# Both MLP products of a two-layer decoder trunk by seven block products each, with the intermediate in HBM

## The chip, the cores and the metric

The kernel runs on one core of a Trainium2 chip, as one launch. The metric is device microseconds from the first to the last instruction, as the median of several executions. The engines are PE (TensorE, matmuls), DVE (VectorE), ACT (ScalarE), POOL (GpSimd) and SP (SyncE, which issues most DMAs). SBUF is the on-chip memory with 128 partitions, PSUM the accumulator memory of TensorE with eight banks, HBM the memory outside the core.

## What is computed

The reference is a trunk of two layers on one sequence of 16 meta tokens and 1024 tokens, D = 1024 features, D_FF = 4096. The first layer (A) has stick-breaking attention, the second (B) differential attention. Each ends in an MLP, and only the MLPs matter here:

```python
def rmsnorm(x, g):
    y = x * lax.rsqrt(jnp.mean(x * x, axis=-1, keepdims=True) + EPS)
    return y * g
...
def squared_relu_mlp(x, g, w_in, w_out):
    h = rmsnorm(x, g)
    return jnp.square(jax.nn.relu(h @ w_in)) @ w_out
...
h = h + squared_relu_mlp(h, mlp_norm_g[layer], mlp_w_in[layer], mlp_w_out[layer])
```

Layer A has 1040 tokens, layer B 1024, since the meta tokens are dropped at the end. All data are float32.

## The kernel before

The stream is kept feature-major (features on partitions, tokens along the free axis) in three chunks of tokens: 400, 384 and 256 in layer A (`CH`), 384, 384 and 256 in layer B (`BCH`). Every product is made in three passes of a faster float format (`mm3`): each operand is split into a high part (`acopy`, a cast on ACT, line 99) and a low part (`tt(..., subtract)`, on DVE, line 113), and high·high, high·low and low·high add up in one PSUM bank (`mm`, line 159). Other helpers are `stt` (line 117, DVE), `ptt` (line 121, an add or subtract on POOL) and `rstd_from` (a matmul with ones, a square root and a reciprocal on line 207).

An MLP is `mlp()`. `out_proj` before it adds the attention's output projection to the stream (tiles `opa`, `opb`), sums squares (`acca`, `accb`, `accx` on POOL) and hands over the split operands X of each chunk, times the norm's gain but not yet over the rms. The weights come in 16 groups of two ff tiles: `load_group` loads 1 MB of `w_in` and 1 MB of `w_out` (tiles `mws`, lines 757 and 778) and splits each as one operation of 128x2048 on ACT and one on DVE (`mwh`, `mwl`). For a group, `hidden` makes the products `mi` per chunk and ff tile, multiplies with 1/rms and applies relu (`rl` on DVE), squares on ACT and splits again (`u`). Then `wout_a` multiplies by the group's `w_out` rows and adds the PSUM result `mo` to the stream `h` in SBUF, or `wout_b` does so in layer B with token-major `my` and `y`. The products of a group's hidden units come ahead of the previous group's `mo`, so TensorE always has something to do. In all, each of the two products of a layer has 2304 matmuls in layer A and 2304 and 1536 in layer B. POOL has no work in an MLP. SP's queue holds only the next groups' loads there, one `w_in` and one `w_out` in turn.

Of the kernel before, what the change touches and what calls it, by code (L numbers as in the profile page):

```python
# [8 lines left out]
F32 = mybir.dt.float32  # L9
# [69 lines left out]
def kernel(ctx: ExitStack, tc: tile.TileContext, inp, out):  # L79
# [112 lines left out]
    accx = const.tile([P, CH[2][1]], F32, name="accx")  # L192
    # token blocks of each chunk (0: the meta tokens)
# [8 lines left out]
    def rstd_from(acc, n, pp, tp, r, tag):  # L202
        """1 / rms per token, on all partitions, from the sums of squares per partition."""
# [5 lines left out]
    def newton(y, v, a):  # L209
        """y = 1/sqrt(v) from y = ln(v): exp(-y/2), then Newton's step."""  # L210
# [5 lines left out]
    def split_row(hv, x, k, gcol):  # L216
        """High and low parts of feature tile k, times the norm's gain, to the act tile x."""
# [14 lines left out]
    # =================== phase 0: tokens to feature-major ===================  # L232
# [98 lines left out]
    def load_o(O, views, k0, k1):  # L331
        """Feature tiles k0..k1 of o^T from scratch; the meta tokens' are never there."""
# [12 lines left out]
    def fill_items(kf, O, views, rows, pp, W, nm):  # L345
        """Closures that add W^T o of the first kf feature tiles to the stream in scratch, chunk by chunk."""
# [11 lines left out]

    def out_proj(W, kf, O, H, views, pp, tp, R, X, gcol, tag, mid):
        """H += W^T O, what the fillers have left of it; X gets each chunk times the gain, R its 1 / rms."""  # L360
        accs = [tp.tile([P, 400], F32, tag="acc", bufs=3, name=f"acc{tag}_{c}") for c in range(3)]

        def step(m, c, off, n, k0):
            ps = pp.tile([P, 512], F32, tag="mm", name=f"op{tag}_{c}_{m}")
            wo_sum(ps, W[m], O, c, off, n, range(k0, KT))
            hv = H[c][:, m, off:off + n]
            tt(hv, hv, ps[:, :n], ALU.add)
            if m == 0:
                act(accs[c][:, :n], hv, AF.Square)
            else:  # L370
                sq = tp.tile([P, 400], F32, tag="sq", bufs=2, name=f"sq{tag}_{c}_{m}")
# [977 lines left out]
```

## Time and profile before

| | |
|---|---|
| median of 3 runs (range) | 2861.45 us (2853.43 to 2861.75) |
| profiled execution | 2852.5 us, span from the first to the last instruction; mean granted clock of TensorE 0.989 |
| busy: PE, DVE, ACT, POOL | 2770.0, 1818.8, 1207.3, 389.6 us |
| MLP of layer A, first `mi` to last `mo` | 725.09 to about 1463 us |
| MLP of layer B, first `mi` to the end | 2135.82 to 2852.5 us |

The engine lines of the page's second part give the busy share of 40 slices of the span, 71.3 us each, in tenths. The chain of waits is followed back from the last instruction: each piece is what the next one waited for.

### The profile page before, as it was taken

What the parts mean: (1) busy time and instruction counts of PE and PEld (TensorE: products, weight loads), DVE (VectorE), ACT (ScalarE), POOL (GpSimd) and SP (SyncE); (2) the same over time, 40 slices, a digit from 0 to 9 for tenths busy, and PEclk for the clock granted to TensorE, in tenths of its full rate; (3) what the DMA queues carried; (4) which work ended last, traced back from release to release, by engine and by line L of the source; (5) the groups of instructions that cost most, each with busy time, mean ns of one, the idle gap of its engine ahead of it and who ended that gap; (6) DMA issues with size and microseconds to landing.
All of it is one profiled execution on the core that took longest, in us unless ns stands there. A gap on an engine that the chain in (4) does not pass through costs nothing.

```text
span 2852.5 us, 45796 instructions
## 1 busy us (share of the span) xinstructions
PE 2770.0 (97%) x17368; PEld 2630.8 (92%) x17368; DVE 1818.8 (64%) x3620; ACT 1207.3 (42%) x2902; POOL 389.6 (14%) x863
## 2 busy tenths in 40 slices
PE   7999999999999999999999999999999999999999
PEld 7898899889999999999989899998899998989988
DVE  6989999885544454544478788888655444354444
ACT  4666666764321121212256667676453222222211
POOL 2211111002000000000144334442030000000000
PEclk9999999999999999999999999999999999999999
DMA  7333333444211111110111112124422111111101
GB/s 210 89 81 83 83 82 82 123 125 134 75 45 45 45 45 45 53 52 30 34 67 49 42 53 57 54 56 137 125 79 80 54 45 45 45 53 51 45 16 59
DMA packets 201565, 197.87 MB, mean 69 GB/s; under 512 B 21433, under 2 KB 185954, under 8 KB 201346
## 3 DMA queue, kind: packets, MB, share of 16 engines
q1 hardware_dynamic: 191986, 190.70, 22.3%
q10 hardware_dynamic: 9360, 4.26, 0.6%
q8 instruction: 137, 2.24, 0.3%
q14 instruction: 82, 0.67, 0.1%
HBM read 131.04 MB, written 29.65 MB: 56 GB/s over the span
## 4 chain that ended last, share of the span: by engine, by line
PE 74%; DVE 7%; ACT 3%; DMA 2%; issue 1%; POOL 1%; SPq 0%; DVEq 0%; POOLq 0%; ACTq 0%
PE mi L159 25%; PE my L159 12%; PE mo L159 12%; PE bpj L159 8%; PE opa L159 2%; PE opb L159 2%; PE sc_b L159 2%; PE avb L159 2%; DVE kp L528 2%; PE pj L159 2%; PE ofb L159 1%; DVE wt L113 1%; PE ptb L162 1%; PE av L159 1%; DVE w L113 1%
## 5 line engine op out<-in xcount | busy, mean ns | idle before, releaser
L159 PE MATMUL mo<-u,mwh 128*128 128x400 f32 (+2 forms) x1536 | 357.8, 321 | 0.0
L159 PE MATMUL mi<-xa,mwh 128*128 128x400 f32 (+2 forms) x1536 | 357.6, 321 | 0.0
L159 PE MATMUL mi<-xb,mwh 128*128 128x384 f32 (+1 forms) x1536 | 353.3, 319 | 0.0
L113 DVE TENSOR_TENSOR h<-h,mo 128x400 f32<-128x400 f32 (+2 forms) x384 | 190.9, 512 | 232.1 <-PE mo L159 231.6
L113 DVE TENSOR_TENSOR y<-y,my 128x512 f32<-128x512 f32 x256 | 174.2, 685 | 232.6 <-PE my L159 231.8
L159 PE MATMUL my<-mwh,u 128*128 128x512 f32 x1024 | 321.6, 393 | 0.0
L159 PE MATMUL pj<-xa,wh 128*128 128x400 f32 (+2 forms) x1152 | 293.7, 334 | 6.9 <-DVE rsa L698 4.9
L159 PE MATMUL bpj<-bwh,xb 128*128 128x384 f32 x1024 | 283.3, 345 | 5.8 <-ACT k L99 4.2
L99 ACT CAST u<-rl 128x384 fp32r<-128x384 f32 (+2 forms) x192 | 92.2, 480 | 439.8 <-PE mo L159 221.0
L159 PEld LDWEIGHTS mo<-u,mwh 128*128 128x128 f32 x1536 | 268.7, 189 | 0.0
L159 PEld LDWEIGHTS mi<-xa,mwh 128*128 128x128 f32 x1536 | 266.5, 188 | 0.1
L159 PEld LDWEIGHTS mi<-xb,mwh 128*128 128x128 f32 x1536 | 264.9, 188 | 1.3
L105 ACT ACTIVATE rl<-rl 128x384 f32<-128x384 f32 (+2 forms) x192 | 92.8, 491 | 407.5 <-DVE rl L117 407.5
L159 PE MATMUL mo<-u,mwl 128*128 128x400 f32 (+2 forms) x768 | 248.5, 324 | 0.0
L159 PE MATMUL mi<-xa,mwl 128*128 128x400 f32 (+2 forms) x768 | 246.7, 321 | 0.0
L159 PE MATMUL mi<-xb,mwl 128*128 128x384 f32 (+1 forms) x768 | 244.4, 318 | 0.0
L159 PEld LDWEIGHTS my<-mwh,u 128*128 128x128 f32 x1024 | 192.7, 188 | 42.5
L99 ACT CAST mwh<-mws 128x2048 fp32r<-128x2048 f32 x64 | 122.1, 1912 | 230.6 <-PE mi L159 224.3
L159 PEld LDWEIGHTS pj<-xa,wh 128*128 128x128 f32 x1152 | 204.3, 195 | 9.1 <-issue 6.6
L117 DVE SCALAR_TENSOR_TENSOR rl<-mi,r 128x384 f32<-128x384 f32 (+2 forms) x192 | 97.2, 513 | 180.4 <-PE mi L159 178.7
L159 PE MATMUL my<-mwl,u 128*128 128x512 f32 x512 | 201.3, 393 | 0.0
L159 PEld LDWEIGHTS bpj<-bwh,xb 128*128 128x128 f32 x1024 | 187.2, 190 | 9.3 <-ACT k L99 6.4
(287 smaller groups left out, 6200.8 us busy)
## 6 DMA issues: line engine op xcount, KB each, us to landing
mws<-in_mlp_w_in_dram SPq DMA_DIRECT2D x32, 1024.0 KB, 5.5
mws<-in_mlp_w_out_dram SPq DMA_DIRECT2D x32, 1024.0 KB, 4.9
o_d<-oh SPq DMA_DIRECT2D x52, 256.0 KB, 2.5
ws<-in_a_w_qkv_dram SPq DMA_DIRECT2D x24, 512.0 KB, 5.7
qb<-q SPq DMA_DIRECT2D x128, 64.0 KB, 2.0
bws<-in_kv_w_dram SPq DMA_DIRECT2D x128, 64.0 KB, 2.0
qbb<-q SPq DMA_DIRECT2D x64, 128.0 KB, 2.4
oa<-o_d SPq DMA_DIRECT2D x4, 1152.0 KB
```

Of the source, the lines that this page charges most:

```text
L99: nc.scalar.copy(out=o, in_=i)
L105: nc.scalar.activation(out=o, in_=i, func=func, **kw)
L113: nc.vector.tensor_tensor(out=o, in0=a, in1=b, op=op)
L117: nc.vector.scalar_tensor_tensor(out=o, in0=a, scalar=s, in1=b, op0=op0, op1=op1)
L159: nc.tensor.matmul(o, lhsT=l, rhs=r, start=start, stop=stop, **kw)
L162: nc.tensor.transpose(out=o, in_=i, identity=ident)
L528: nc.vector.tensor_tensor_scan(out=rv, data0=rv, data1=rv, initial=1.0, op0=ALU.mult, op1=ALU.bypass)
```

## The change

Both products of each MLP are made by one level of Strassen's scheme in Winograd's form: operands are cut into 2 × 2 blocks, seven block products replace eight, and sums of blocks are made before and after. `mlp_stage` replaces `out_proj` and `mlp` in both layers.

**First product.** The stream H is normed in place (`normed`), `ops7(c)` makes the seven operand blocks of token half c (high and low parts, ten DVE and two POOL operations and seven casts of 1040 columns). A unit is one token half c and one pair j of ff tiles (columns 128 and 128 of `w_in`), so 32 units per layer, and `w_in` is loaded twice. Per unit, `w_sums` makes four sums of 128x512 on POOL (`s0`..`s3`), `w_split` splits seven blocks of 128x512 (`w1`..`w7`, ACT and DVE), the seven products have 12 matmuls of 260 columns each (256 in layer B) in three banks, `relu2` and a square make blocks of the squared relu, POOL combines them in four operations of 260 columns to the seven blocks U that the second product needs, and U goes to HBM (`u_d`, 932 KB).

**Second product.** After all units, in the order `PROD2` of seven products, with 16 pairs of ff tiles each (112 steps): the U block `b` is read back (266 KB), the weight block is a resident one (`r11`, `ra0`..`ra2`, 12.6 MB loaded for this) or `a12`, read each time (256 KB), or a sum made on POOL (products 6, 7 and 5; one or two `ptt` of 512 columns, and for 5 also an add on DVE). Both are split on ACT and DVE, and the matmuls of the step are 24 of 260 columns (A) or 12 of 512 (B). After each product, `half_add` adds its PSUM banks to the stream.

```diff
-        def load_group(g):
-            W = w0 if g == 0 else load_in(li, q, g)
-            ws = q[0].tile([P, 2048], F32, tag="ws", bufs=2, name=f"mws{li}_{g}_1")
...
-            acopy(h, ws)
-            tt(l, ws, f(h), ALU.subtract)
...
+    PROD1 = (1, 5, 6, 2, 7, 3, 4)
+    PROD2 = (2, 1, 6, 7, 4, 5, 3)
+    NPAIR = NF // 2
...
+        def wop(nm):
+            return mw.tile([P, 2, 520], F32R, tag="wop", bufs=10, name=nm)
+
+        def srow(nm):
+            return mw.tile([P, 520], F32, tag="s", bufs=5, name=nm)
+
+        def raw(nm):
+            return mw.tile([P, 4, 256], F32, tag="ws", bufs=4, name=nm)
...
+            rstd_from(accs[c][:, :n], n, pp, tp, R[:, s], f"{tag}{c}")
+            for k in range(KT):
+                stt(H[:, k, s], H[:, k, s], gains[:, gcol + k:gcol + k + 1], R[:, s], ALU.mult, ALU.mult)
...
+        def w_sums(u):
+            k0, k1 = raws[u]
+            a11, a21, a12, a22 = k0[:, :, :P], k0[:, :, P:], k1[:, :, :P], k1[:, :, P:]
...
+            ptt(s[0], a21, a22, ALU.add)
+            ptt(s[1], s[0], a11, ALU.subtract)
+            ptt(s[2], a11, a21, ALU.subtract)
+            ptt(s[3], a12, s[1], ALU.subtract)
+            sums[u] = {1: a11, 2: a12, 3: s[3], 4: a22, 5: s[0], 6: s[1], 7: s[2]}
...
+            if u + 2 < nu:
+                w_load(u + 2)
+            if u + 1 < nu:
+                w_sums(u + 1)
...
+            for i in PROD1:
+                ps = {1: b1, 6: b1, 7: b1, 4: b1, 5: b2, 3: b2, 2: b3}[i]
+                h, l = wops.pop((u, i))
...
+                if i == 1:
+                    acopy(t1, b1)
+                elif i == 6:
+                    acopy(u2, b1)
+                elif i == 2:
+                    tt(t1, b3, t1, ALU.add)
+                    relu2(ublk(1), t1)
+                elif i == 7:
+                    acopy(u3, b1)
+                    tt(u3, b2, u3, ALU.add)
+                    relu2(ublk(3), u3)
+                elif i == 3:
+                    tt(u2, b2, u2, ALU.add)
+                    relu2(b12, u2)
+                    ptt(ublk(5), b12, ublk(1), ALU.subtract)
+                    ptt(ublk(7), ublk(3), b12, ALU.subtract)
+                    ptt(ublk(6), ublk(3), ublk(5), ALU.subtract)
+                elif i == 4:
+                    nc.vector.tensor_scalar(out=m21, in0=b1, scalar1=0.0, scalar2=None, op0=ALU.max)
+                    act(ublk(2), m21, AF.Square)
+                    ptt(ublk(4), ublk(2), ublk(6), ALU.subtract)
+                if u + 1 < nu:
+                    w_split(u + 1, i)
+            nc.sync.dma_start(out=u_d[:, j, :, c * nn:(c + 1) * nn], in_=U)
...
+        ops7(1, X7[1])
+        st_h.close()
...
+            nc.sync.dma_start(out=H, in_=h_d)
+        for u in range(NPAIR, nu):
+            unit(u, nu)
+        st_x.close()
...
+        for q in range(4):
+            nc.sync.dma_start(out=r11[q], in_=wr[0, :, 4 * q:4 * q + 4, :512])
...
+        for i in PROD2:
...
+            for fi in range(NPAIR):
...
+                bs = braw(f"b{tag}_{i}_{fi}")[:, :half]
+                nc.sync.dma_start(out=bs, in_=u_d[:, fi, i - 1, :half])
+                if i in (2, 5):
+                    a12 = braw(f"a12{tag}_{i}_{fi}")[:, :512]
+                    nc.sync.dma_start(out=a12, in_=wr[1, :, fi, :512])
...
+                    if i == 7:
+                        ptt(a, a11, a21, ALU.subtract)
+                    else:
+                        ptt(a, a21, a22, ALU.add)
+                        if i == 6:
+                            ptt(a, a, a11, ALU.subtract)
+                        else:
+                            tt(a11, a11, a12, ALU.add)
+                            ptt(a11, a11, a, ALU.subtract)
+                w, b = wop(f"wa{tag}_{i}_{fi}"), wop(f"wb{tag}_{i}_{fi}")
+                for t, s, n in ((w, a, 512), (b, bs, half)):
+                    acopy(t[:, 0, :n], s)
+                    tt(t[:, 1, :n], s, f(t[:, 0, :n]), ALU.subtract)
...
+            half_add(mh, nh, pss)
```

The order of instructions shows three places. POOL first, before the change: at the start of layer A's MLP it goes from the last sums of squares (`acca`) straight to the weights of layer B's attention (`bws0`).

```order
L121 TENSOR_TENSOR acca_2_8521<-acca_2_8521,sqa_2_5_9037 128x256 [waits Activation_49,Pool_49]
L121 TENSOR_TENSOR acca_2_8521<-acca_2_8521,sqa_2_6_9070 128x256 [waits Activation_49,Pool_49]
L121 TENSOR_TENSOR acca_2_8521<-acca_2_8521,sqa_2_7_9099 128x256 [waits Activation_49,Pool_49]
L1024 TENSOR_SCALAR bws0_0_15573<-bws0_0_15573,gains_70 128x128 [waits DMAHW4_49,DMAHW5_49,DMAHW3_49,DMAHW6_49,DMAHW2_49,DMAHW7_49,DMAHW1_49,DVE_49]
L1024 TENSOR_SCALAR bws0_0_15573<-bws0_0_15573,gains_70 128x256 [waits DMAHW1_49,DMAHW0_49]
```

POOL after the change, one of the 32 units of the same stage: the sums of unit 12's weights stand between the combinations of unit 8's blocks `ua_8`.

```order
L121 TENSOR_TENSOR ua_8_10338<-cta_8_3_10342,ua_8_10338 128x260 [waits DMAHW4_49,DVE_49]
L121 TENSOR_TENSOR ua_8_10338<-ua_8_10338,cta_8_3_10342 128x260
L121 TENSOR_TENSOR ua_8_10338<-ua_8_10338 128x260 [waits Pool_49]
L121 TENSOR_TENSOR s0a_12_10753<-mwsa_12_0_10607,mwsa_12_1_10609 128x512 [waits DMAHW6_49,DMAHW0_49,Activation_49]
L121 TENSOR_TENSOR ua_8_10338<-ua_8_10338 128x260 [waits Activation_49,Pool_49]
L121 TENSOR_TENSOR s1a_12_10754<-s0a_12_10753,mwsa_12_0_10607 128x512 [waits DVE_49,Pool_49]
L121 TENSOR_TENSOR s2a_12_10755<-mwsa_12_0_10607 128x512 [waits DVE_49]
L121 TENSOR_TENSOR s3a_12_10756<-mwsa_12_1_10609,s1a_12_10754 128x512 [waits DVE_49,Pool_49]
```

So eight operations a unit stand where there was none, each with inputs in SBUF. DVE, after the change, in such a unit: splits of unit 9's weights between the evacuations of units 6 and 7 (`ct`, `ua`).

```order
L113 TENSOR_TENSOR w1a_9_10357<-mwsa_9_0_10181,w1a_9_10357 128x512 [waits DMAHW5_49,Activation_49]
L113 TENSOR_TENSOR cta_6_1_10056<-mia_6_1_10052,cta_6_1_10056 128x260 [waits PE_49]
L117 SCALAR_TENSOR_TENSOR cta_6_3_10058<-cta_6_1_10056 128x260 [waits DVE_49]
L925 TENSOR_SCALAR cta_6_4_10059<-mia_6_0_10051 128x260
L113 TENSOR_TENSOR w5a_9_10372<-s0a_9_10327,w5a_9_10372 128x512 [waits Activation_49]
L113 TENSOR_TENSOR cta_7_0_10197<-mia_7_2_10195,cta_7_0_10197 128x260 [waits Activation_49]
L117 SCALAR_TENSOR_TENSOR ua_7_10196<-cta_7_0_10197 128x260 [waits DMAHW1_49,DVE_49,Pool_49]
L113 TENSOR_TENSOR w6a_9_10388<-s1a_9_10328,w6a_9_10388 128x512 [waits Activation_49]
```

DVE before, in the same stage: one split of 128x2048, and otherwise additions and relus that read PSUM (`mo`, `mi`), and splits of `u`.

```order
L113 TENSOR_TENSOR h1_2_8481<-h1_2_8481,mo1_2_7_10091 128x256 [waits PE_49]
L113 TENSOR_TENSOR u0_2_2_1_9904<-rl0_2_2_1_9901,u0_2_2_1_9904 128x256 [waits Activation_49]
L113 TENSOR_TENSOR mwl0_3_1_10108<-mws0_3_1_10105,mwh0_3_1_10107 128x2048 [waits DMAHW6_49,Activation_49]
L117 SCALAR_TENSOR_TENSOR rl0_3_0_0_10136<-mi0_3_0_0_10111,r1_0_8471 128x400 [waits DVE_49,PE_49]
L113 TENSOR_TENSOR u0_3_0_0_10139<-rl0_3_0_0_10136,u0_3_0_0_10139 128x400 [waits Activation_49]
```

The third place is SP's queue at the end of layer A's first product, after the change. `ua_31` is the last unit's block, and the reads of the second product's first steps (`ba_2_0`, `a12a_2_0`) come behind the resident weights.

```order
L1007 DMA ra0a_13735<-in_mlp_w_out_dram 128x6x512 [waits DMAHW3_49,PE_49]
L1007 DMA ra0a_13735<-in_mlp_w_out_dram 128x6x512 [waits DMAHW4_49]
L930 DMA u_d_74<-ua_31_13619 128x7x260 [waits DMAHW5_49,Pool_49]
L1004 DMA r11a_0_13731<-in_mlp_w_out_dram 128x4x512 [waits DMAHW6_49]
L1004 DMA r11a_1_13732<-in_mlp_w_out_dram 128x4x512 [waits DMAHW7_49,DMAHW2_49]
L1004 DMA r11a_2_13733<-in_mlp_w_out_dram 128x4x512 [waits DMAHW5_49,DMAHW1_49,DMAHW0_49]
L1004 DMA r11a_3_13734<-in_mlp_w_out_dram 128x4x512 [waits DVE_49]
L1019 DMA ba_2_0_13756<-u_d_74 128x520
L1022 DMA a12a_2_0_13758<-in_mlp_w_out_dram 128x512 [waits DMAHW3_49]
L1019 DMA ba_2_1_13790<-u_d_74 128x520 [waits DMAHW4_49]
```

Before the change, SP has at this stage only `mws` loads in turn, none behind more than 2 MB. In the middle of the first product, `ra1` (3.1 MB) and the stream (`hqa`, 4.3 MB, read back from `h_d`) likewise stand ahead of the next unit's weight loads and of the write of U:

```order
L1007 DMA ra1a_13736<-in_mlp_w_out_dram 128x6x512 [waits PE_49]
L1007 DMA ra1a_13736<-in_mlp_w_out_dram 128x6x512 [waits DMAHW6_49]
L971 DMA hqa_11488<-h_d_71 128x8320 [waits DMAHW7_49,Pool_49]
L856 DMA mwsa_19_1_11634<-in_mlp_w_in_dram 128x4x256 [waits DMAHW0_49,DVE_49]
L856 DMA mwsa_20_0_11774<-in_mlp_w_in_dram 128x4x256 [waits DMAHW1_49,DVE_49,Pool_49]
L930 DMA u_d_74<-ua_15_11334 128x7x260 [waits DMAHW2_49,Pool_49]
```

These 7.4 MB were not on the queue before.

## Rows read from the trace of the kernel before

**Rows 1.** Page, parts 1 and 2: busy us by engine, and GpSimd's busy tenths.

```profile
PE 2770.0 (97%) x17368; PEld 2630.8 (92%) x17368; DVE 1818.8 (64%) x3620; ACT 1207.3 (42%) x2902; POOL 389.6 (14%) x863
...
POOL 2211111002000000000144334442030000000000
```

**Rows 2.** Chain of waits, in order of time: start us, us, what.

```profile
719.39 5.69 PE opa L159 x48
725.09 13.00 PE mi L159 x72
...
793.77 22.85 PE mi L159 x144
816.62 22.82 PE mo L159 x144
...
2203.61 22.32 PE mi L159 x144
2225.93 22.09 PE my L159 x96
```

**Rows 3.** Windows: stretch, its us, busy us of each engine (instructions), PEclk, DMA share, GB/s.

```profile
20.00:50.00 30.00, 28.25 (x169) 26.77 (x170) 26.64 (x44) 11.95 (x25) 11.49 (x9) 0.95 0.93 253
650.00:700.00 50.00, 48.80 (x288) 47.46 (x287) 27.64 (x43) 22.14 (x37) 14.67 (x14) 1.00 0.57 186
1180.00:1300.00 120.00, 120.00 (x760) 120.00 (x759) 61.87 (x110) 26.25 (x38) 0.00 (x0) 1.00 0.14 45
1459.00:1464.00 5.00, 5.00 (x31) 5.00 (x30) 4.78 (x19) 3.30 (x11) 0.29 (x1) 0.66 0.50 180
```

**Rows 4.** Timeline of TensorE in layer A's MLP: start us, us, what, count.

```profile
1099.76 0.52 PE L159 MATMUL mo<-u,mwh 128*128 128x384 f32 x2
...
1107.66 0.39 PE L159 MATMUL mo<-u,mwh 128*128 128x256 f32 x2
...
1112.27 0.39 PE L159 MATMUL mo<-u,mwh 128*128 128x256 f32 x2
```

**Rows 5.** Timeline of GpSimd in layer A's output projection, in brackets idle before and releaser.

```profile
681.05 1.04 POOL L121 TENSOR_TENSOR acca<-acca,sqa 128x400 f32<-128x400 f32 x1 [1.11 <-ACT sqa L105]
...
719.86 0.74 POOL L121 TENSOR_TENSOR acca<-acca,sqa 128x256 f32<-128x256 f32 x1 [1.25 <-ACT sqa L105]
```

**Rows 6.** Groups by shape, VectorE and ScalarE: busy us, mean ns | idle before, releasers.

```profile
L99 ACT CAST wt<-pt 128x512 fp32r<-128x512 f32 x160 | 90.2, 587 | 57.5 <-PE av L159 51.1 <-PE pt L162 6.0
...
L113 DVE TENSOR_TENSOR h<-h,mo 128x256 f32<-128x256 f32 x128 | 52.2, 418 | 20.1 <-PE mo L159 19.6
...
L113 DVE TENSOR_TENSOR wl<-ws,wh 128x1024 fp32r<-128x1024 f32 x24 | 29.2, 1216 | 1.2 <-POOL wh L124 1.0
...
L113 DVE TENSOR_TENSOR u<-rl,u 128x256 fp32r<-128x256 f32 x64 | 26.9, 421 | 8.3 <-ACT u L99 8.3
```

**Rows 7.** Timeline of GpSimd and VectorE at the end of layer A.

```profile
1437.10 9.46 POOL L121 TENSOR_TENSOR accx<-accx,sqx 128x400 f32<-128x400 f32 x7 [22.75 <-ACT sqx L105]
...
1437.02 0.57 DVE L113 TENSOR_TENSOR xb<-h,xb 128x400 fp32r<-128x400 f32 x1
...
1438.86 0.56 DVE L113 TENSOR_TENSOR h<-h,mo 128x400 f32<-128x400 f32 x1
1439.34 0.94 DVE L113 TENSOR_TENSOR xb<-h,xb 128x400 fp32r<-128x400 f32 x1
...
1440.21 0.56 DVE L113 TENSOR_TENSOR h<-h,mo 128x400 f32<-128x400 f32 x1
```

**Rows 8.** The six instructions of line 207: ns min/median/max, first and last start, forms.

```profile
L207 DVE RECIPROCAL r<-r x6: 1746/2552/2652, 704.2 to 2152.4; 128x384 f32<-128x384 f32 x3, 128x256 f32<-128x256 f32 x2, 128x400 f32<-128x400 f32 x1
```

**Rows 9.** Page, part 6, DMA issues: count, KB each, median us to landing.

```profile
mws<-in_mlp_w_in_dram SPq DMA_DIRECT2D x32, 1024.0 KB, 5.5
```

**Rows 10.** Timeline of TensorE at the end of layer A's MLP.

```profile
1458.23 0.83 PE L159 MATMUL rsx<-ones,accx 128*128 128x2 f32 x6 [3.06 <-POOL accx L121]
...
1460.67 0.63 PE L159 MATMUL mo<-u,mwh 128*128 128x256 f32 x2
...
1461.31 0.63 PE L159 MATMUL mo<-u,mwh 128*128 128x256 f32 x2
```

More of the change, by code (lines that the diff above doesn't have):

```diff
@@ L184 @@
     vm_d = dr.tile([HA, NM, P], F32, name="vm_d")
+    u_d = dr.tile([P, NF // 2, 7, T // 2], F32, name="u_d")
+    y_d = dr.tile([SEQ, D], F32, name="y_d")
     gqk = const.tile([P, 4, HD], F32, name="gqk")
@@ L191 @@
     rsx = const.tile([P, 9], F32, name="rsx")
-    accx = const.tile([P, CH[2][1]], F32, name="accx")
     BL = ((1, 2, 3, 0), (4, 5, 6), (7, 8))
@@ L357, in fill_items @@
         return [lambda m=m, v=v: item(m, *v) for v in views for m in range(len(W))]
[L359 to L371, printed above, removed]
-                act(sq[:, :n], hv, AF.Square)
-                ptt(accs[c][:, :n], accs[c][:, :n], sq[:, :n], ALU.add)
-        def split(c, off, n):
-            x = act_tile(c, f"x{tag}")
-            for m in range(KT):
-                split_row(H[c][:, m, off:off + n], x, m, gcol)
-            X.append(x)
-        def rstd(c, off, n):
-            rstd_from(accs[c][:, :n], n, pp, tp, R[c][:, :n], f"{tag}{c}")
-        for m in range(NMF):
-            for v in views:
-                step(m, *v, kf)
-        mid()
-        for i, v in enumerate(views):
-            for m in range(NMF, KT):
-                step(m, *v, 0)
-                if i and m == NMF + 2:
-                    rstd(*views[i - 1])
-            split(*v)
-        return lambda: rstd(*views[-1])
     rebalance(EBA)
@@ new lines, with norms @@
+    XB, accd, pend = [], set(), []
+    acc_ = {}
+    def norms(pp, tg, c):
+        blocks = [(b, max(0, NM + P * (b - 1))) for b in BL[c]]
+        rs = pp.tile([P, 512], F32, tag=tg, name=f"rsx{c}")
+        for i, (b, o) in enumerate(blocks):
+            w = P if b else NM
+            mm(rs[:w, 2 * i:2 * i + 2], acc_["x"][:, o:o + w], ones[:, 0:2], i == 0, i == len(blocks) - 1, skip_group_check=True)
+        if c == 0:
+            tc.keep_in_program_order(nc.scalar.preload_act_table_set("natural_log_exp_and_others"))
+        full = [b for b in BL[c] if b]
+        b0 = full[0]
+        for p, q, i, k in ((P, slice(b0, b0 + len(full)), 0, len(full)), (NM, slice(0, 1), len(full), 1)):
+            if p == NM and c:
+                continue
+            v, y, t = (const.tile([P, 4], F32, tag="nx", bufs=6, name=f"nx{c}_{p}_{j}")[:p, :k] for j in range(3))
+            nc.vector.tensor_scalar(out=v, in0=rs[:p, 2 * i:2 * (i + k):2], scalar1=1.0 / D, scalar2=EPS,
+                                    op0=ALU.mult, op1=ALU.add)
+            ln = nc.scalar.activation(out=y, in_=v, func=AF.Ln)
+            if c == 0 and p == P:
+                tc.keep_in_program_order(ln)
+            newton(y, v, t)
+            nc.vector.tensor_copy(out=rsx[:p, q], in_=y)
@@ new lines, in epilogue_a @@
+    def epilogue_a(i, mh, nh, H, mw, hq, pp):
+        if i in (1, 4):
+            return
+        accx = acc_["x"] = acc_["x"] if acc_ else hq.tile([P, T], F32, name="accx")
+        for c in range(3 if i == 5 else 0):
+            XB.append(act_tile(c, "xb"))
+        quarters = [(0, 0), (1, 0), (1, 1)] if i == 5 else [(0, 1)]
+        for mh, nh in quarters:
+            for c, a, n in spans(520 * nh, 520):
+                t0 = CH[c][0] + a
+                for m in range(4 * mh, 4 * mh + 4):
+                    hv = H[:, m, t0:t0 + n]
+                    acopy(XB[c][:, 0, m, a:a + n], hv)
+                    tt(XB[c][:, 1, m, a:a + n], hv, f(XB[c][:, 0, m, a:a + n]), ALU.subtract)
+                    acc = accx[:, t0:t0 + n]
+                    if nh not in accd:
+                        act(acc, hv, AF.Square)
+                    else:
+                        sq = mw.tile([P, 520], F32, tag="s", bufs=5, name=f"sqx{c}_{nh}_{m}")[:, :n]
+                        act(sq, hv, AF.Square)
+                        ptt(acc, acc, sq, ALU.add)
+                    if m == 4 * mh + 3 and t0 + n == 520 * nh + 520:
+                        accd.add(nh)
+                nc.sync.dma_start(out=h_d[:, 4 * mh:4 * mh + 4, t0:t0 + n], in_=H[:, 4 * mh:4 * mh + 4, t0:t0 + n])
+        if i == 3:
+            for c in range(3):
+                norms(pp, "mm", c)
@@ L907 @@
+    mlp_stage(0, WO, inp["a_w_o"][0], None, O, CHV, KFA, G_M0, 0, stw.close, lambda *a: None, epilogue_a)
     rebalance(EBB)
@@ new lines, in to_rows @@
+    def to_rows(H, ci, pp, srow):
+        c, off, n = BCH[ci]
+        t0 = CH[c][0] + off - NM
+        for b in range(t0 // P, (t0 + n) // P):
+            for k4 in range(2):
+                ps = pp.tile([P, 512], F32, tag="mm", name=f"ty{b}_{k4}")
+                for k in range(4):
+                    tr(ps[:, k * P:(k + 1) * P], H[:, 4 * k4 + k, b * P:(b + 1) * P], idf)
+                y = srow(f"yr{b}_{k4}")[:, :512]
+                evac(y, ps)
+                nc.sync.dma_start(out=y_d[b * P:(b + 1) * P, 512 * k4:512 * k4 + 512], in_=y)
@@ L1324, with epilogue_b @@
+    def epilogue_b(i, mh, nh, H, mw, hq, pp):
+        for b in range(4 * nh, 4 * nh + 4):
+            s = slice(512 * mh, 512 * mh + 512)
+            nc.sync.dma_start(out=out[0, b * P:(b + 1) * P, s], in_=H[:, b, s])
+    mlp_stage(1, WO, inp["b_w_o"][0], gains[:, G_SUB:G_SUB + 1], O, BCH, KFB, G_M1, NM, stw.close, to_rows, epilogue_b)
 _INS = ["x", "meta_tokens", "a_norm_g", "a_w_qkv", "a_w_o", "kv_norm_g", "kv_w", "kv_k_norm_g", "b_norm_g", "b_w_q",
```

410 lines of the change are left out of this document (223 added, 187 removed).

## The prediction

> **What bounds the kernel now.** I began with the page's first two parts [rows 1]: TensorE is busy 97% of the span, GpSimd 14%, and GpSimd's line of forty slices is empty where the two MLPs stand (slices 11 to 19 and 31 to 40). Then the chain of waits [rows 2]: between the output projection and the end of each layer it is TensorE alone, one piece of `mi` and one of `mo` or `my` per weight group, end to end. So these stages are limited by TensorE, and everything else there hides behind it; VectorE is half busy and GpSimd not at all [rows 3]. The price of a matmul comes from TensorE's timeline [rows 4]: 15 rows of two and 15 of one matmul of 384 columns fill the 7.90 us from 1099.76 to 1107.66, 45 at 175.6 ns, and 13 and 13 such rows of 256 columns the 4.61 us up to 1112.27, 39 at 118.2 ns. The slope gives 120.0 ns for 260 columns. For 512 columns, 22.09 us over 96 matmuls is 230.1 ns [rows 2].
>
> **What TensorE saves.** Before: 16 groups of 22.85 + 22.82 us in layer A and of 22.32 + 22.09 us in layer B [rows 2], 1441 us. After: each unit of the first product has 7 × 12 = 84 matmuls, so 32 × 84 × 120.0 ns = 323 us in A and 32 × 84 × 118.2 ns = 318 us in B. The second product has 112 steps (7 products × 16 pairs of ff tiles) of 24 matmuls of 260 columns in A, 323 us, and of 12 of 512 columns in B, 309 us. Sum 1272 us, **−169 us**: 7/8 in count, a little less for 260-column matmuls in place of 400.
>
> **What the first product now asks of GpSimd and VectorE.** Each unit gives GpSimd four sums of 512 columns (`s0`..`s3`) and four of 260 (the blocks of U), where it did nothing before. VectorE gets seven splits of 512 and three of 260 with both inputs in SBUF, and four of 260 with one input in PSUM. Alone, neither is too slow. GpSimd's 400 and 256 columns take 1.04 and 0.74 us [rows 5], that is 0.21 us + 2.08 ns a column: 1.27 us for 512, 0.75 for 260, 8.1 us a unit. VectorE's two-input form takes 421 ns for 256 and 1216 ns for 1024 columns [rows 6], 0.156 us + 1.035 ns a column: 4.8 + 1.3 us, and 4 × 0.42 us for the PSUM reads, 7.8 us. Both lie under TensorE's 10.08 us.
>
> But they don't run beside each other. At the end of layer A there is a stretch [rows 7] in which GpSimd adds seven times 400 columns without a gap, 9.46 us, so 1.35 us each against 1.04 alone. VectorE alternates there between adds from PSUM, which keep 0.56 us, and two-input splits of 400, which take 0.94 us against 0.57 just before GpSimd began. One period of one GpSimd add and one split is 1.345 us, where whole durations would be 1.04 + 0.57 = 1.61. So GpSimd and the two-input form take turns column by column, and only their fixed parts overlap: 400 × 1.035 ns = 0.41 us for VectorE leave 0.93 us for GpSimd, 2.33 ns a column. For a unit that is (4 × 512 + 4 × 260) × 2.33 ns = 7.19 us and (7 × 512 + 3 × 260) × 1.035 ns = 4.52 us, **11.7 us** as the low end; whole durations (8.08 + 6.1) give **14.2 us** as the high end. I take 12.3 us: the stretch is nearer to the low end, but in the unit `s1` waits for `s0`, `s3` for `s1`, and U's last blocks for VectorE, so there are small gaps. Against 10.08 and 9.93 us that is 32 × 2.2 + 32 × 2.3 = **+144 us** (107 to 266). So the first product falls to the pair of GpSimd and VectorE, and nothing hides it.
>
> The Trainium skill, "SBUF — State Buffer", section "Who interferes with whom", says that a VectorE instruction with two SBUF inputs contends with a GpSimd one that reads SBUF, that one with at most one SBUF input does not, and calls the shared ports an exclusive lock. Rows 7 agree on who contends; on the lock they show 1.345 us and not the 1.61 of strict turns, and the sum above goes by the rows.
>
> Its other work has cover. ScalarE has seven casts of 512 (0.59 us [rows 6]) and four of 260, at most 6.5 of 12.3 us. The DMA has 1.05 MB in and 0.93 MB out per unit; at the 253 GB/s at 0.93 busy or the 186 at 0.57 [rows 3], so 272 to 326 GB/s full, 6.1 to 7.3 us.
>
> **The second product.** For product 6 each step gives GpSimd two sums of 512 and VectorE splits of 512 and 520: (1024 × 2.33 + 1032 × 1.035) ns = 3.45 us against TensorE's 2.88 (A) and 2.76 us (B). For product 5 an add of 512 more: 3.99 us. The excess over 16 steps is 9.1 + 17.8 us in A and 11.0 + 19.7 us in B, 58 us; product 7 has one sum and lies under TensorE, and the ten operand buffers let some steps run ahead: **+45 us** (25 to 58).
>
> **The head of each MLP.** Before, TensorE went from `opa` to `mi` without a gap [rows 2], since 1/rms was only needed after the product. After, the stream is normed before it. From feature tile 4 of the last chunk: a reciprocal of 2.55 us [rows 8], eight two-input normings of 384 columns, 0.55 us by the fit, ten VectorE and two GpSimd operations of 1040 columns that take turns, 10.8 + 4.8 us: 22.5 us. Three projections of that chunk, 24 matmuls each at 5.69/48 us, cover 8.5 us; the rest, 14 us per layer, is paid, though unit 0 starts on the first block: **+28 us** (16 to 34).
>
> **The middle.** `ops7(1)` adds the same 15.6 us to a pair that is already the limit: 31 us over both layers. On SyncE's queue `ra1` (3.1 MB) and H (4.3 MB) stand ahead of unit 19's second weight half and unit 15's U: 7.4 MB at 272 to 326 GB/s is 23 to 27 us, and about a unit's 12.3 us of loads is ahead: 12 us per layer. **+55 us** (20 to 80).
>
> **Between the products.** `r11` takes the space of the first product's tiles and `ra0` that of its operands, so they load when TensorE and VectorE are done with them; `b` and `a12` of the first step stand behind them on the queue: 3.15 + 0.93 + 4.19 + 0.5 = 8.8 MB, 27 to 32 us, and a first cast and split of 1.2 us. VectorE, ScalarE and TensorE have nothing to do in it. 31 us per layer, **+62 us** (54 to 68).
>
> **Small things.** In product 2 both operands come from HBM through four buffers, two a step; a 1 MB load lands 5.5 us after its issue [rows 9], and two steps of 2.9 us are all the lead that these smaller ones have: **+10** (0 to 20). At each of 14 product ends `half_add` stands between TensorE and its banks; the first bank comes free after one add of 0.42 us [rows 6], with hand-overs 1.2 us: **+17** (10 to 30). Norms that ran in layer B's attention now end layer A: **+3** (0 to 6).
>
> **Sum.** 144 + 45 + 28 + 55 + 62 + 10 + 17 + 3 = +364, less 169: +195 us on the profiled 2852.5 us, 3048 us. The median of the runs, 2861.45, is 9 us above that execution, so **3057 us**. With all low ends (+232) it is 2924, with all high ends (+561) 3253 us.
>
> **Rivals.**
> *GpSimd and VectorE don't hinder each other here*, because operations miss each other or the 260-column ones are spread out. Then the 144 and 45 us vanish, 25 of the middle and 10 of the head: −224, 2833 us, **faster**. For: neither has more than 8.1 of 10.08 us. Against: rows 7, at a load like this one's. It decides only if more than 205 of the 224 us go.
> *Strict turns*, each instruction whole: 14.2 us a unit (+122) and 3.9 and 4.6 us for a step of products 6 and 5 (+47): 3179 us with the first alone, 3226 us with both. Rows 7 speak against it (1.345, not 1.61), though that stretch has no operations that wait for each other. The "exclusive lock" of the Trainium skill's page "SBUF — State Buffer" would, taken to the letter, be this rival.
> *The loads are hidden*: the space for `r11` and H comes free early enough, so that 24 of the middle and most of the 62 us go: 2975 us, still slower. Against it are the waits on PE and VectorE in SyncE's order.
> *The clock falls.* TensorE now has a gap of 2 us in 12. After the idle 3.06 us before `rsx`, 256-column matmuls went from 118 to 213 ns (three from 1460.67 to 1461.31) for 3 us [rows 10], the 1.2 GHz level; the granted clock was 0.66 there [rows 3]. Held for the whole first product it would be 84 × 213 ns = 17.9 us a unit, +360, 3415 us. For gaps of 2 us spread evenly nothing here shows such a fall: from 20 to 50 us TensorE is busy 28.25 of 30 us at 0.95 [rows 3].
>
> **How the numbers follow.** Forecast 0.58; no hindrance 0.10; strict turns 0.17; hidden loads 0.10; clock 0.05. The range 2890 to 3230 us holds the forecast, the hidden loads and nearly all of strict turns; about 2 in 10 lie outside. A measurement of this kernel tells about 0.3% from no change. Only the second case reaches below that: faster 0.10; between it and the rest 0.03 for the same; slower 0.87.
>
> **What would show it.** In the first product a period of about 12.3 us a unit, GpSimd busy nearly throughout with 512-column sums of some 1.7 us, and TensorE idle 2 us a unit, released by VectorE. Between the last `mi` and the first `mo` a gap of about 31 us, released by DMA, twice. In product 5 a period near 4 us a step. Wrong would be: 10.1 us a unit (no hindrance), over 13.5 (strict turns), a clock under 0.9 there, or a gap under 15 us between the products.

## The result, and the profile after

The changed kernel takes 3038.5 us (median of 4 runs, 3035.08 to 3045.02) beside 2857.44 us of the kernel before on the same chip: ratio 1.0632, 95% interval 1.0609 to 1.0655, 6.3% slower. The forecast was 3057 us. The profiled execution has a span of 3034.2 us, 181.7 us more than the one before.

The page of the kernel after (parts 1 and 2), beside [rows 1]: GpSimd's busy time has grown from 389.6 to 1319.6 us, and TensorE, which had been busy 97% of the span, has fallen to 89%. GpSimd's line has most of its 7s and 8s just where TensorE's falls to 7s and 8s.

```profile
PE 2695.3 (89%) x18328; PEld 2535.8 (84%) x18328; DVE 2375.2 (78%) x4028; ACT 1518.6 (50%) x3601; POOL 1319.6 (43%) x1545
...
PE   7999999998787885999889999999978878869998
...
POOL 2211111014777774082644344332147778832732
```

From the first and last matmuls of each stage in the trace (their starts and ends), the 181.7 us stand here:

| stretch | before | after | difference |
|---|---|---|---|
| start to the end of layer A's output projection | 725.1 | 730.2 | +5.1 |
| MLP of layer A: wait ahead of it, first product, wait, second product | 739.1 | 8.0 + 439.6 + 27.8 + 341.4 | +77.7 |
| end of layer A to the end of layer B's output projection | 663.4 | 688.1 | +24.7 |
| MLP of layer B, in the same parts | 724.9 | 12.3 + 433.4 + 26.8 + 322.9 (and 3.7 to the end) | +74.2 |

So the second products are faster than before (365 and 353 us, 16 groups of [rows 2] each), the first ones slower by 74 and 76 us, and the rest is lost around them.

The windows of the kernel after over nine units of the first product, over the wait between the products and over most of products 2, 1 and 6 of layer A (columns as in [rows 3]): in the units no engine is full, TensorE 85%, VectorE 83%, GpSimd 78%; in the wait TensorE does nothing and the DMA moves 341 GB/s at a share of 0.99; in the second product TensorE is full.

```profile
814.80:932.10 117.30, 100.20 (x756) 98.34 (x757) 97.45 (x127) 50.33 (x99) 91.40 (x72) 0.93 0.48 153
...
1177.80:1205.60 27.80, 0.05 (x2) 0.01 (x1) 1.75 (x4) 1.56 (x3) 15.12 (x14) 0.58 0.99 341
...
1210.00:1345.00 135.00, 135.00 (x1127) 135.00 (x1126) 94.25 (x116) 59.20 (x107) 48.90 (x30) 1.00 0.48 134
```

One unit in the timelines of the kernel after, GpSimd, VectorE and TensorE:

```profile
846.19 1.74 POOL L121 TENSOR_TENSOR s1a<-s0a,mwsa 128x512 f32<-128x512 f32 x1
847.90 1.50 POOL L121 TENSOR_TENSOR s2a<-mwsa 128x512 f32<-128x512 f32 x1
...
850.52 1.71 POOL L121 TENSOR_TENSOR s3a<-mwsa,s1a 128x512 f32<-128x512 f32 x1
...
848.15 1.80 DVE L113 TENSOR_TENSOR w3a<-s3a,w3a 128x512 fp32r<-128x512 f32 x1
849.87 1.23 DVE L113 TENSOR_TENSOR w4a<-mwsa,w4a 128x512 fp32r<-128x512 f32 x1
851.03 1.75 DVE L113 TENSOR_TENSOR w1a<-mwsa,w1a 128x512 fp32r<-128x512 f32 x1
852.70 0.41 DVE L113 TENSOR_TENSOR cta<-mia,cta 128x260 f32<-128x260 f32 x1
...
849.41 1.60 PE L159 MATMUL mia<-x1a,w3a 128*128 128x260 f32 x12
853.26 1.97 PE L159 MATMUL mia<-x0a,w1a 128*128 128x260 f32 x12 [2.25 <-DVE cta L113]
855.03 2.80 PE L159 MATMUL mia<-x0a,w6a 128*128 128x260 f32 x12
```

GpSimd's 512 columns take 1.50 to 1.74 us (1.27 forecast alone, 1.7 beside VectorE), and a split of 512 up to 1.80 us where it would take 0.69. The products of several units are interleaved on TensorE: at 851 us it has done product 3 of one unit, and next on its queue is the first product (`w1a`) of a unit three later, which takes the PSUM bank that was just filled; VectorE reads this bank (`cta<-mia`) only at 852.70, behind three splits that GpSimd has slowed. After that wait of 2.25 us the next matmuls are slow: in the windows from 840.7 to 849.4 and from 855.0 to 858.4 us the granted clock is 1.00 and 0.58, near its lower level of 1.2 GHz, and twelve matmuls take 2.80 us in place of 1.60. In layer A, units without such a fall take 12.5 to 12.7 us, units with one 13.2 to 13.6; the mean is 12.96 us in layer A and 12.80 in layer B (from the first matmul of unit 5 to that of unit 16, as in the runs below).

### The profile page after: what moved, and what is told of

It is laid out like the page before. It is cut to its first block, busy times and chain, and to the rows that moved or that the text cites. A ratio compares the mean times of both kernels' runs of the same rounds, so it can differ in the third digit from the quotient of the medians.

```text
span 3034.2 us, 51503 instructions
## 1 busy us (share of the span) xinstructions
PE 2695.3 (89%) x18328; PEld 2535.8 (84%) x18328; DVE 2375.2 (78%) x4028; ACT 1518.6 (50%) x3601; POOL 1319.6 (43%) x1545
## 3 DMA queue, kind: packets, MB, share of 16 engines
q1 hardware_dynamic: 340978, 367.87, 40.3%
## 5 line engine op out<-in xcount | busy, mean ns | idle before, releaser
L159 PE MATMUL moa<-wba,waa 128*128 128x260 f32 x2688 | 329.6, 286 | 39.6 <-ACT wba L99 27.8
L159 PEld LDWEIGHTS moa<-wba,waa 128*128 128x128 f32 x2688 | 328.0, 191 | 41.1 <-ACT wba L99 29.8
L159 PE MATMUL mob<-wab,wbb 128*128 128x512 f32 x1344 | 315.7, 396 | 34.1 <-ACT wbb L99 26.8
L159 PEld LDWEIGHTS mob<-wab,wbb 128*128 128x128 f32 x1344 | 252.8, 189 | 96.7 <-ACT wbb L99 29.5
L494 DVE TENSOR_TENSOR_SCAN kp<-kp 128x144 f32<-128x144 f32 (+7 forms) x128 | 185.4, 1454 | 11.6 <-ACT kp L105 10.8
L159 PE MATMUL pj<-xa,wl 128*128 128x384 f32 (+2 forms) x576 | 192.7, 334 | 0.0
L159 PE MATMUL bpj<-bwl,xb 128*128 128x384 f32 x512 | 174.8, 341 | 0.0
L105 ACT ACTIVATE w<-sc,rsa 128x392 f32<-128x392 f32 (+4 forms) x224 | 121.6, 544 | 33.2 <-PE sc L159 31.7
L105 ACT ACTIVATE kp<-sc,rsa 128x392 f32<-128x392 f32 (+4 forms) x224 | 120.2, 538 | 11.9 <-DVE w L113 11.8
L159 PEld LDWEIGHTS pj<-xa,wl 128*128 128x128 f32 x576 | 112.1, 195 | 0.5
```

The source lines that it names most:

```text
L105: nc.scalar.activation(out=o, in_=i, func=func, **kw)
L159: nc.tensor.matmul(o, lhsT=l, rhs=r, start=start, stop=stop, **kw)
L494: nc.vector.tensor_tensor_scan(out=rv, data0=rv, data1=rv, initial=1.0, op0=ALU.mult, op1=ALU.bypass)
```

## The experiments

The theory (A): VectorE's two-input operations and GpSimd's take turns, and this sets the unit. The rival (B): the wait for the PSUM bank alone does.

**Without GpSimd in the first product.**

```diff
-            ptt(s[0], a21, a22, ALU.add)
-            ptt(s[1], s[0], a11, ALU.subtract)
-            ptt(s[2], a11, a21, ALU.subtract)
-            ptt(s[3], a12, s[1], ALU.subtract)
-            sums[u] = {1: a11, 2: a12, 3: s[3], 4: a22, 5: s[0], 6: s[1], 7: s[2]}
+            sums[u] = {1: a11, 2: a12, 3: a12, 4: a22, 5: a21, 6: a11, 7: a21}
...
-                    ptt(ublk(5), b12, ublk(1), ALU.subtract)
```

> This kernel leaves out all of GpSimd's work in the first product (the four weight sums are replaced by plain blocks, the four combinations of U by copies of other blocks in the write to HBM), so its output is not the reference's; VectorE, ScalarE, TensorE and the bytes moved stay. Theory A (GpSimd and VectorE's two-input operations take turns, and this sets the unit): the 512-column splits fall to 0.69 us, a unit from about 12.9 us to 10.1 to 10.8 us, the first product from 440 and 433 us to 330 to 350 us, the whole time by about 180 us to about 2860 us. Theory B (TensorE waits at each unit's start for a PSUM bank that VectorE reads behind three splits, and this alone sets the unit): the wait falls only from 2.3 to about 1.5 us, a unit takes 11.5 us or more, the time falls by less than 90 us.

Measured: 2880.2 us, 158 us less; first products of 365.7 and 359.8 us, a unit 10.93 and 10.76 us. Windows over five units, and VectorE's splits there:

```profile
846.70:901.30 54.60, 51.57 (x420) 50.65 (x421) 37.40 (x71) 27.93 (x57) 0.00 (x0) 1.00 0.57 183
...
L113 DVE TENSOR_TENSOR w3a<-mwsa,w3a 128x512 fp32r<-128x512 f32 x5 | 3.4, 685 | 0.0
```

The slowest of the seven splits falls from 1664 ns (mean over nine units of the kernel after) to 685 ns, the mean of all seven from 1160 to 690 ns, with the same work on VectorE; 148 us of the first products go. Theory B asked for 11.5 us or more: it falls as the sole cause. Theory A's numbers were too good (units of 10.1 to 10.8 us, products of 330 to 350 us): of a unit, some 0.8 us over its matmuls is not GpSimd's.

**Banks of their own.** The three accumulators of a unit are rotated over four, three and one banks.

```diff
-            b1, b2, b3 = (pp.tile([P, 512], F32, tag="mm", name=f"mi{tag}_{u}_{i}")[:, :nn] for i in range(3))
+            b1, b2, b3 = (pp.tile([P, 512], F32, tag=f"m{i + 1}", bufs=(4, 3, 1)[i], name=f"mi{tag}_{u}_{i}")[:, :nn] for i in range(3))
```

> The three accumulators of a unit get banks of their own (four, three and one of the eight), so that a unit's first product no longer takes the bank that the product just before it has filled; all work stays. Theory A: the pair of GpSimd and VectorE stays at 11.7 us or more a unit; only its gaps and the clock's falls go, 12.0 to 12.4 us a unit, -35 to -60 us, about 2990 us. Theory B: TensorE no longer waits, a unit takes 10.1 to 10.8 us, -130 us or more, 2900 us or less.

Measured: 3017.0 us, 1.0558 (1.0541 to 1.0576). Windows over four units:

```profile
874.90:924.90 50.00, 42.56 (x336) 40.91 (x336) 48.53 (x57) 21.92 (x45) 41.16 (x33) 1.00 0.50 160
```

Now every unit takes 12.5 us (means 12.49 and 12.41), the granted clock is 1.00 (0.93 with the waits of 2.25 us), and VectorE is at 97%: 12.1 us a unit, where its operations undisturbed would take the 7.8 us of the prediction, and the rest is their lengthening beside GpSimd. The bank and the clock were worth 0.4 to 0.5 us a unit, some 28 us over the 64 units as the means have it; the pair keeps the rest. The whole time fell by 21 us, less than the 35 expected; the middle takes 5 us longer there in each layer (80.5 and 80.1 us from unit 16 to 21, where the kernel after has 75.4 and 74.9).

**Splits with one SBUF input.** With the same banks, the second operand of the splits is a constant block in PSUM.

```diff
-            tt(l, s, f(h), ALU.subtract)
+            tt(l, s, B3[0][:, 384:512].unsqueeze(1).broadcast_to([P, 4, P]), ALU.subtract)
```

> The accumulators of a unit as in the run with banks of their own, and the seven splits of a unit subtract a constant block in PSUM in place of the high part in SBUF (the low parts are wrong by that, the output is not the reference's). GpSimd has all its work, VectorE as many operations of the same length; only the number of SBUF inputs of the splits changes from two to one. Theory A (two-input operations and GpSimd take turns): the splits fall to about 0.69 us, GpSimd's sums of 512 to about 1.3 us, a unit from 12.5 to 10.1 to 10.8 us, -110 to -150 us against the run with banks of its own. Rival (GpSimd's chain of dependent sums, or the number of operations, sets the unit): it stays above 11.8 us.

Measured: 2922.7 us, a unit 11.17 and 11.01 us. One sum and one split in the run with banks of its own (four units of layer A), then windows and groups of this run (five units of layer B):

```profile
L121 POOL TENSOR_TENSOR s1a<-s0a,mwsa 128x512 f32<-128x512 f32 x4 | 7.0, 1742 | 0.0
...
L113 DVE TENSOR_TENSOR w7a<-s2a,w7a 128x512 fp32r<-128x512 f32 x4 | 7.1, 1780 | 0.0
```

```profile
2300.10:2354.90 54.80, 52.62 (x423) 50.39 (x422) 39.29 (x71) 27.73 (x56) 39.86 (x41) 1.00 0.58 181
...
L121 POOL TENSOR_TENSOR s1b<-s0b,mwsb 128x512 f32<-128x512 f32 x5 | 6.5, 1295 | 0.4
...
L113 DVE TENSOR_TENSOR w7b<-s2b,b3b 128x512 fp32r<-128x512 f32 x5 | 3.4, 677 | 0.0
```

All operations are there, on the same engines, and both engines run at or near their undisturbed durations: the seven splits take 673 to 677 ns (mean 1326 with two SBUF inputs), the four sums 1295 to 1422 ns (mean 1608), where 1.27 us was worked out from [rows 5]. Beside the place of the second operand one thing changes: a split no longer waits for ScalarE's cast. That can't be the gain, since VectorE was idle for only 1.5 of 50 us in the run with banks of its own. So the cause is the second SBUF input, not the number of operations. The gain, 94 us against the run with banks of its own, is less than the 110 expected, and a unit lies between theory A's 10.8 us and the rival's 11.8: three two-input operations of 260 are left, and a unit stays 1 us over its matmuls.

**Three two-input operations fewer.** With banks of its own and late loads (below), relu times itself goes to ScalarE.

```diff
-                stt(o, x, 0.0, x, ALU.max, ALU.mult)
+                act(x, x, AF.Relu)
+                act(o, x, AF.Square)
```

> The run with banks of their own and late loads, and three two-input operations of 260 columns per unit (relu times itself) go from VectorE to ScalarE as two operations each. By theory A the pair loses 3 x 260 x 1.035 ns = 0.8 us and their switches: a unit of 12.5 goes to 11.4 to 11.8 us, -45 to -70 us, about 2920 us. Rival: ScalarE's longer queue (8 us a unit, in order, with waits for TensorE) makes the casts late, and the unit stays at 12.3 us or more.

Measured: 2981.5 us, where the run without it has 2980.9; a unit 12.26 and 12.32 us. The rival's number came. Windows over four units, and GpSimd's timeline in one:

```profile
874.90:924.90 50.00, 44.43 (x345) 41.95 (x345) 30.59 (x46) 32.43 (x71) 41.33 (x34) 1.00 0.51 166
...
879.35 0.74 POOL L121 TENSOR_TENSOR ua<-cta,ua 128x260 f32<-128x260 f32 x1 [1.98 <-ACT cta L105]
```

VectorE's busy time has fallen from 48.53 to 30.59 of 50 us, but GpSimd now waits 1.98 us a unit for ScalarE, some of whose casts wait for TensorE in turn (they write into the ten operand buffers that TensorE reads). So 11.7 us, the pair's throughput, was not what a unit comes to. The waits suggest a loop through four engines, in which the pair's slowness is the largest piece; more operand buffers, which would test it, were not tried.

**Late loads.** The second product begins with product 1; `r11` and `ra` come between its steps, H in eight pieces.

```diff
-    PROD2 = (2, 1, 6, 7, 4, 5, 3)
+    PROD2 = (1, 6, 7, 4, 2, 5, 3)
...
+                if i == 1 and fi in (1, 5, 9):
+                    tc.keep_in_program_order(r11_load(fi // 4 + 1))
+                if i == 1 and fi in rest:
+                    tc.keep_in_program_order(ra_load(*rest[fi]))
```

> The loads of the resident weights come one by one between the second product's steps, which begin with product 1 in place of 2 (so that the 4.2 MB of r11 stream along), and the stream H comes back in eight pieces, one per unit. If the stall between the products is the 8.8 MB ahead of the first step's operands, it falls from 27 us to 8 to 14 us in both layers, and the middle by up to 10 us each: -30 to -50 us in all, about 3000 us. If it is the drain of the last unit (its U to HBM and back), it stays above 20 us. Rival for the middle: ops7's 15.6 us of VectorE and GpSimd make it, and it stays at 11 us.

> Both edits of the two runs before together. Their gains are in different places, so they should add: by theory A 2940 to 2960 us, by theory B 2870 us or less.

Measured: 3009.9 us, 1.0533 (1.0518 to 1.0549), and 2980.9 us, 1.0436 (1.042 to 1.0452), with both edits. TensorE's first step of the second product in the kernel after and in the run with late loads:

```profile
1205.60 1.67 PE L159 MATMUL moa<-wba,waa 128*128 128x260 f32 x6 [27.75 <-ACT wba L99]
```

```profile
1187.97 2.32 PE L159 MATMUL moa<-wba,waa 128*128 128x260 f32 x9 [13.22 <-ACT wba L99]
```

The wait falls from 27.8 and 26.8 to 13.2 and 13.1 us: half of it was the queue of resident weights. In what is left in layer B, 3.9 us pass until GpSimd has finished the last U, whose write stands ahead of the first reads on SyncE's queue, and the first read takes 7.46 us (chain of waits of the run with late loads):

```profile
2667.28 0.73 POOL ub L121
2668.03 0.36 SPq L930
...
2669.05 7.46 DMA bb<-u_d
```

The first step does not need that last U: in the kernel with three waits out (below) its operands have space of their own and come earlier, and this wait is gone.

The middle did not get shorter: from unit 16 to unit 21 it is 75.4 us in layer A of the kernel after and 75.0 here, so the loads of the stream don't make it; that leaves `ops7`, which no run took out alone. The two edits together give 58 us, a little more than their sum (21 and 29 us alone), and still miss theory A's 2940 to 2960 us, since both gave less than expected.

**Seven products only in the second product.** The first is made of eight plain block products (96 matmuls, four splits, no weight sums), with the late loads.

```diff
+                for kh in range(2):
+                    h, l = wops[u, wi[kh]]
+                    x = x7[xi[kh]]
+                    for k in range(4):
+                        mm3(ps, h[:, k], l[:, k], x[:, 0, k], x[:, 1, k], kh == 0 and k == 0, kh == 1 and k == 3)
```

> Only the second product keeps seven products: the first is made of eight plain block products per unit (96 matmuls in place of 84), with four splits in place of seven and no weight sums; GpSimd keeps the four combinations of U; the loads of resident weights and of H are spread as in the run with late loads. If GpSimd and VectorE's pair is what made the first product slow, TensorE sets it again: 11.5 us a unit, first products of 370 to 380 us where 437 and 436 were, no stall in the middle, 2860 to 2890 us, about as long as the kernel before all changes. If something else of the unit (its writes and loads, the order of evacuations) is the limit, a unit stays near 12.5 us and the time near 3000 us.

Measured: 2852.6 us, 0.9992 (0.9981 to 1.0003), as long as the kernel before and a little under the range. Windows over 17 units of layer A: TensorE is full, GpSimd and VectorE are at 29% and 39%, and VectorE's splits are back at 693 ns.

```profile
850.00:1050.00 200.00, 200.00 (x1674) 200.00 (x1673) 77.75 (x139) 70.52 (x140) 57.53 (x71) 1.00 0.60 189
```

A unit takes 11.5 us with 96 matmuls, where 84 took 12.96: a seventh more work for TensorE is faster than the sums that save it.

**Three waits out of that kernel.** First operands in space of their own, the operand of product 3 made in place, one norm moved back.

```diff
+                if i == 2:
+                    a = a12 = braw(f"a12{tag}_{i}_{fi}")[:, :512]
...
+                    ptt(a11, a11, a12, ALU.add)
...
+                elif i == 7:
+                    ptt(a11, a11, a21, ALU.subtract)
+                    a = a11
+                elif i == 4:
+                    ptt(a11, a11, a22, ALU.subtract)
```

> The run with eight block products in the first product, and three waits taken out that its trace still shows: the first steps' operands of the second product get space of their own, so that they load before the first product ends (12.7 and 12.3 us of stall to 1 to 3 us each); the operand of the last product is made in place by one GpSimd operation in each of three products, in place of three operations on GpSimd and VectorE in product 5 (60.5 and 53.2 us there, where the others take 46 and 44.6, to about 47 and 46 us, and a12 is read once); the last chunk's norm goes back into layer B's attention (some 4 us of a 15 us tail). In sum -35 to -50 us, 2800 to 2820 us, 1.2 to 1.8% faster than the kernel before. Rival: the loads of the resident weights, which still start only when the first product ends, come too late for product 1's fifth step, and half of the stall comes back there: 2820 to 2835 us.

Measured: 2839.3 us, 0.9946 (0.9927 to 0.9966). This is slower than both ranges. The waits between the products are gone, and product 5 takes 46.8 and 44.4 us; of the waits, only 1.9 and 2.3 us come back, at product 1's fifth step, where the rival put them. But product 6 takes 62.4 and 60.1 us. GpSimd's order had changed with the edit: it ran sums of products 7 and 5 ahead between those of product 6.

```diff
+        def kptt(o, x, y, op):
...
+            tc.keep_in_program_order(nc.gpsimd.tensor_tensor(out=o, in0=x, in1=y, op=op))
```

> The run before lost in product 6 what it won between the products: 62.3 and 60.1 us where 46.8 and 46.2 were, since GpSimd ran the in-place sums for products 7 and 5 ahead, between those of product 6. Here GpSimd's sums of the second product keep the order of the products; nothing else changes. If this running ahead was the cause, product 6 goes back to 46 to 49 us in both layers, -25 to -30 us, 2808 to 2820 us, 1.2 to 1.6% faster than the kernel before. Rival: the loads of the resident weights (8.4 MB that can only start when the first product ends) made product 6 slow; then it stays above 55 us and the time at 2830 us or more.

Measured, with GpSimd's sums held in the order of the products: 2827.0 us, 0.9923 (0.9902 to 0.9944), 0.8% faster than the kernel before. TensorE at the change of products and at the end of product 6, and GpSimd and VectorE there:

```profile
1094.12 1.12 PE L159 MATMUL moa<-wba,waa 128*128 128x260 f32 x8
...
1199.81 1.43 PE L159 MATMUL moa<-wba,waa 128*128 128x260 f32 x5 [7.51 <-DVE hqa L113]
...
1175.05 20.38 POOL L972 TENSOR_TENSOR r11a<-r11a,ra1a 128x512 f32<-128x512 f32 x12
...
1197.58 1.75 DVE L113 TENSOR_TENSOR wba<-ba,wba 128x520 fp32r<-128x520 f32 x1
1199.26 0.75 DVE L113 TENSOR_TENSOR hqa<-hqa,moa 128x260 f32<-128x260 f32 x2
```

The time lies between the two forecasts. Product 6 is at 56.5 and 56.2 us, not at 46: running ahead was a part of it. The rest has the size that the rival gave, but another reason: at the end of product 6 TensorE waits for VectorE, not for a load. Its last steps take 3.4 us, since the splits go at 1.7 us in turn with GpSimd's sums for product 7, and then it waits 7.5 us for `half_add`, whose adds stand on VectorE behind four such splits. That this would go with another order on VectorE was not tried.

## Why the prediction was right, point by point

The measured 3038.5 us lie 18.5 us under the forecast, well within its range, and what was named as the largest loss, the pair of GpSimd and VectorE in the first product, is what the runs show. Term by term:

- **TensorE, −169 us**: right for the matmuls. Steps of the second product take 2.88 and 2.79 us (46.1 and 44.6 us over 16) where 24 × 120 ns and 12 × 230 ns gave 2.88 and 2.76, and the eight-product unit takes 11.5 us for 96 × 120 ns. But the old MLPs took 1460 us up to their last matmul where the sum put 1441, so 19 us went with them that had no term.
- **First product, +144 us**: right in place and mechanism, too small. 32 × (12.96 − 10.08) + 32 × (12.80 − 9.93) = 184 us. That the two engines hinder each other is shown by the two runs that remove it (10.8 to 10.9 and 11.0 to 11.2 us a unit). What the sum lacked is the bank that TensorE waits for and the clock's falls behind that wait, shown by the run with banks of its own (0.4 to 0.5 us a unit). The fall of the clock had been given 0.05 and as all or nothing; it came in part. The step "small gaps" was the weak one: with fewer two-input operations the unit did not follow the pair's throughput.
- **Rival without hindrance**: fell with the unit of 12.96 us and the run with the PSUM operand; its price of 10.08 us a unit was not reached by any run either.
- **Strict turns** (14.2 us a unit): fell, units 5 to 16 of layer A stay under 13.7 us, and their mean under 13.0.
- **Head, +28**: too small. The waits ahead of the first matmul are 8.0 and 12.3 us, but the head goes on behind them: the first 168 matmuls, two units' worth, take 38.8 and 40.3 us where the mean pace would be 25.9 and 25.6. In layer A VectorE is full all this time, and TensorE's granted clock is 0.81 (window below). So 48 us, over the high end of 34; that unit 0 can start on the first block hid less than the sum thought.

```profile
738.20:777.00 38.80, 26.62 (x171) 25.36 (x172) 38.80 (x44) 16.61 (x31) 22.42 (x14) 0.81 0.23 69
```

- **Middle, +55**: 22 us, since 75.4 us from unit 16 to 21 is 10.6 over five units of 12.96, and 74.9 in layer B is 10.9 over five of 12.80. The step that failed is that nothing makes up for `ops7`: after unit 16 (26.9 us), units 17 and 18 take only 9.4 and 10.5 us in layer A. VectorE and GpSimd work a few units ahead of TensorE's evacuations, and this lead may be what pays; that was not tested. The loads, 24 of the 55, cost next to nothing there, as the run with late loads shows.
- **Between the products, +62**: 27.8 and 26.8 us. The chain of waits before layer B's second product shows the two landings that the term named, the last U's at 9.75 us and `a12`, behind the resident weights, at 10.11 us:

```profile
2684.68 9.75 DMA u_d<-ub
...
2696.23 10.11 DMA a12b<-in_mlp_w_out_dram
...
2707.56 2.50 PE mob L159 x5
```

- **Second product, +45, +10 and +17**: 18.8 and 13.7 us over its matmuls, 32 in place of 72. Product 6 in layer A cost nothing (46.1 us, like product 1): GpSimd makes its first sum 10 us before TensorE comes to it. Product 5 costs 13 and 7 us (59.2 and 51.4 us, 17.8 and 19.7 expected). In layer B it has three steps at 4.0 us, the 3.99 of the sum, and one at 3.7, the others being ahead of it; in layer A two steps of 7.7 and 7.9 us make most of it.
- **Norms, +3**: 13.7 us more than before between the last `mo` and layer B's first projection (`bpj`). After the last matmul TensorE waits 5.63 and 3.91 us for GpSimd's sums of squares and 2.33 us for VectorE:

```profile
1553.31 1.44 PE L159 MATMUL rsx<-ones,accx 128*128 128x2 f32 x6 [5.63 <-POOL accx L121]
1558.67 1.01 PE L159 MATMUL rsx<-ones,accx 128*128 128x2 f32 x4 [3.91 <-POOL accx L121]
1562.01 0.45 PE L159 MATMUL bpj<-bwh,xm 128*48 128x256 f32 x1 [2.33 <-DVE nx L117]
```

What was too small: first product +40, head +20, norms +11, and two pieces that had no term, 8 us in the two output projections (70.7 and 71.6 us against 67.3 and 67.2) and 8 us in the stages before them (1.7 in layer A, 6.6 in layer B). What was too large: second product −40, middle −33, between the products −7, and the 19 us that went with the old MLPs. Together that is −13 on the 195 us: the total is nearer than its parts, and so near by luck. What makes the output projections and the stages before them longer was not tried.

## What to carry to other kernels

Count the vector work of a scheme that saves matmuls by sums, and look where its operands lie: GpSimd beside two-input VectorE work costs both. Try such a scheme product by product: here it pays where operands can be made ahead and TensorE still sets the step (−24 and −31 us in the second products; 0.8% of the whole in the last run), and not where every step needs seven splits and eight sums. Look, too, at which bank a next product takes: the one just filled is the last to be read.

## What was not expected of the hardware

The turns of GpSimd and VectorE are not always even. In product 5 of layer A one GpSimd operation of 512 columns stands for 8.13 us, while VectorE runs two-input operations back to back at their undisturbed 0.68 us; then both slow down to about 1.75 us for 512 columns each:

```profile
1464.16 8.13 POOL L121 TENSOR_TENSOR r11a<-r11a,aa 128x512 f32<-128x512 f32 x1 [2.37 <-DVE r11a L113]
...
1466.24 0.68 DVE L113 TENSOR_TENSOR waa<-aa,waa 128x512 fp32r<-128x512 f32 x1
...
1470.48 0.67 DVE L113 TENSOR_TENSOR waa<-aa,waa 128x512 fp32r<-128x512 f32 x1
1471.08 1.77 DVE L113 TENSOR_TENSOR wba<-ba,wba 128x520 fp32r<-128x520 f32 x1
```

The Trainium skill, "SBUF — State Buffer", section "Who interferes with whom", calls the ports that the two share an exclusive lock and says that issue order decides who blocks. Here the GpSimd operation stands through eight VectorE operations that all begin after it, so the order of issue alone does not tell it, though the profile's spans on GpSimd are rough. What decides between the two patterns no run shows.
